# Shorter sine arguments, grouped sines and fewer rotary products in the first stage of a hybrid encoder layer

## The chip, the cores and the metric

The kernel runs on one core of one Trainium2 chip. The core has a matrix engine (PE, with its weight loads, PEld), a vector engine (DVE), a scalar engine that evaluates functions (ACT), a general engine (POOL), and a queue that issues most transfers (SP). Each engine takes its instructions in order. The metric is the device time of one execution in microseconds. Times of single instructions and stages are from one profiled execution; the comparison is between medians of several executions.

## The reference

One encoder layer over 2048 tokens of width 1024. After an RMS norm, one projection gives queries, keys and values of a grouped-query attention with 8 query heads and 2 key heads of 64, and the three streams of a Hyena operator of width 512. Then come the output projection, a residual, an MLP with squared ReLU of width 4096, a residual and a last norm. Two parts matter here. Queries and keys are normalised by head and turned by an axial rotary table:

```
def _rotate(x, cos, sin):
    x1, x2 = jnp.split(x, 2, axis=-1)
    ...
    return jnp.concatenate([x1 * cos - x2 * sin, x2 * cos + x1 * sin], axis=-1)
```

And the long filters of the Hyena operator come from a small network with three sine layers of width 64, evaluated at 2048 positions:

```
    h = jnp.sin(freq * (z @ w1 + b1))
    h = jnp.sin(freq * (h @ w2 + b2))
    h = jnp.sin(freq * (h @ w3 + b3))
    h = h @ w4
```

The frequencies are large enough that the arguments leave the range of one turn, so each has to be brought back to it.

## The kernel before

The kernel is a chain of stages that each free their memory for the next: `qkv_proj` with the filter network beside it; `attention` with the filter's taps and the Hyena projection beside it; the transforms of the filters; two convolutions; the output mix; the MLP. The transforms, the convolutions and the mix run in the order in which they are written (`in_order`). **The first two stages don't:** a builder that models the durations of the instructions gives each engine its order, and an instruction that is ready by the model may be placed ahead of one that stands earlier in the program.

`qkv_proj` goes over 16 token tiles of 128. A tile is loaded and squared for its norm (L204), scaled (L206), turned by eight transposes (L215), split into a high and a low half (`ah` by ACT, L217, `al` by DVE, L218), and multiplied with the split weights: 24 matmuls of 512 columns for the queries, 24 of 256 columns for keys and values (L164 to L166). `taken` copies the result out of the accumulator (L233 to L240), and POOL multiplies it with the gains and with the cosines (L245, L247). `norm_rope` sums the squares by head (L252), takes the reciprocal root (`rstd_steps`, L114 to L121, with a square root on ACT, L116), multiplies the swapped halves with the sines (L259, four products of 160 elements), adds them (L261), scales (L262) and splits (L264 on ACT, L265 on DVE). `finish` turns queries and keys (L279), copies them out on ACT (`qs`, L281) and stores them (L287). The steps of several tiles overlap.

Beside this runs `filter_hidden`, a generator that the loop over tiles pumps once a tile. Its 16 steps each make one argument of 128 partitions by 512 positions: a matmul (L1239), then `sin_argument` on DVE. There the bias is added and the frequency multiplied (L1197), the number of turns is rounded by adding and subtracting a large constant (L1198, L1200), the turns are subtracted in two parts (L1202, twice), and the result is clamped (L1203). `sines` (L1234) runs on ACT over four arguments at a time: four of the first layer, four of the second, twice four of the third. The last layer's results are split into `hc` (L1263 on ACT, L1264 on DVE). Arguments and sines share the six buffers of the tile `sx`.

ACT holds the tables of one set of functions. Where it changes from the square root to the sine or back, the trace has an ACT_TABLE_LOAD.

After the loop, SP issues the loads of the next stage, among them the keys (L422), small vectors of the convolution (L336, L339) and the weights of the Hyena projection (L357). Attention then adds up the weights of each block on POOL (`sum`, L489). Late in that stage, POOL and DVE also fold the taps for the transform (L1398, L1399) as soon as they are loaded back (L1381).

Of the kernel before, what the change touches and what calls it, by code (L numbers as in the profile page):

```python
# [14 lines left out]
AF = mybir.ActivationFunctionType  # L15
ALU = mybir.AluOpType
# [4 lines left out]
P = 128  # L21
# [16 lines left out]
def f32(ap):  # L38
    return ap.bitcast(F32)
# [85 lines left out]
def rstd_from_root(*args):  # L125
    got = []
    pump(rstd_steps(*args, got), 3)
    return got[0]
# [43 lines left out]
def qkv_proj(k, pa, ps, side):  # L172
    nc, a = k.nc, k.a
    x, w_in = a["x"][0], a["w_in"][0]
# [54 lines left out]
    NH = NQ + NKV  # L229
# [20 lines left out]
    def norm_rope(t, y, z, w, cs):  # L250
        ss = pa.tile([P, NH], F32, name="ss")
        nc.vector.tensor_reduce(out=ss[:], in_=z[:], axis=AX.X, op=ALU.add)  # L252
        r = rstd_from_root(k, pa, ss[:], HD, NH, "qr")
        yv = y[:].rearrange("p h (a b e) -> p h a b e", a=2, b=2)
        zv = z[:].rearrange("p h (a b e) -> p h a b e", a=2, b=2)
        sv = cs[:, 1].rearrange("p (a b e) -> p a b e", a=2, b=2)
        for ax in range(2):
            for b in range(2):
                nc.vector.tensor_mul(out=zv[:, :, ax, b], in0=yv[:, :, ax, 1 - b],  # L259
                                     in1=sv[:, ax, b].unsqueeze(1).to_broadcast([P, NH, 16]))  # L260
        nc.vector.tensor_add(out=w[:], in0=w[:], in1=z[:])  # L261
        nc.vector.tensor_mul(out=w[:], in0=w[:], in1=r[:].unsqueeze(2).to_broadcast([P, NH, HD]))  # L262
        hl = pa.tile([P, NH, 2, HD], F32R, name="hl", bufs=FL)
        nc.scalar.copy(out=hl[:, :, 0], in_=w[:])  # L264
        nc.vector.tensor_sub(out=hl[:, :, 1], in0=w[:], in1=f32(hl[:, :, 0]))  # L265
        return hl
# [32 lines left out]
    for i in range(-1 - XL, NT + FL):  # L299
        if i == 13:  # L300
            k.first = load_q(k, 0), {(0, b): load_k(k, k.early, 0, b, 4) for b in range(2)}, load_v(k, k.early, 0)
        if 1 < i + XL + 2 < NT:
            xt[i + XL + 2] = load_x(i + XL + 2)
        e = i - FL
        ending = 0 <= e < NT
        if ending:
            finish(e, *hl[e], 0)
        if 1 < i < NT:
            oq[i] = project(*aT[i], 0, QW)
        if ending:  # L310
            finish(e, *hl[e], 1)
        if 0 <= i + 1 < NT:
            aT[i + 1] = turned(i + 1, xs.pop(i + 1))
        if 0 <= i + XL + 1 < NT:
            xs[i + XL + 1] = normed(i + XL + 1, xt.pop(i + XL + 1))
        if 0 <= i + 1 < 2:
            oq[i + 1] = project(*aT[i + 1], 0, QW)
        pump(side, 1 if i > 0 else 0)
        if ending:
            finish(e, *hl.pop(e), 2)  # L320
        if 0 <= i < NT:
            okv = project(*aT.pop(i), QW, 256)
        if 0 <= i - 1 < NT:
            hl[i - 1] = twice(norm_rope(i - 1, *yz.pop(i - 1)))
        if 0 <= i < NT:
            yz[i] = taken(i, oq.pop(i), okv)
# [859 lines left out]


MAGIC = 1.5 * 2.0 ** 23
TWO_PI = (6.28125, 0.0019353071795864769)
PI_IN = 3.1415925  # L1190


def sin_argument(k, pool, ps, bias, freq):
    nc = k.nc
    x = pool.tile([P, 512], F32, name="sx", bufs=6)
    n = pool.tile([P, 512], F32, name="sn", bufs=2)
    nc.vector.tensor_scalar(out=x[:], in0=ps, scalar1=bias, scalar2=freq, op0=ALU.add, op1=ALU.mult)  # L1197
    nc.vector.tensor_scalar(out=n[:], in0=x[:], scalar1=1.0 / (2.0 * math.pi), scalar2=MAGIC,  # L1198
                            op0=ALU.mult, op1=ALU.add)
    nc.vector.tensor_scalar(out=n[:], in0=n[:], scalar1=MAGIC, scalar2=None, op0=ALU.subtract)  # L1200
    for c in TWO_PI:
        nc.vector.scalar_tensor_tensor(out=x[:], in0=n[:], scalar=-c, in1=x[:], op0=ALU.mult, op1=ALU.add)  # L1202
    nc.vector.tensor_scalar(out=x[:], in0=x[:], scalar1=PI_IN, scalar2=-PI_IN, op0=ALU.min, op1=ALU.max)  # L1203
    return x


# [3 lines left out]
def filter_hidden(k, f1, ps):  # L1210

    nc, a = k.nc, k.a
    H = FH
    w1 = f1.tile([66, P], F32, name="w1")
    w2 = f1.tile([P, P], F32, name="w2")
    w3 = f1.tile([P, 2, P], F32, name="w3")
    fb = f1.tile([P, 3], F32, name="fb")
    fr = f1.tile([P, 1], F32, name="fr")
    for t in (w1, w2, w3):
        nc.gpsimd.memset(t[:], 0.0)  # L1220
    for i in range(2):
        h = slice(i * H, (i + 1) * H)
        nc.sync.dma_start(out=w1[33 * i:33 * (i + 1), h], in_=a["filt_w1"][0])
        nc.sync.dma_start(out=w2[h, h], in_=a["filt_w2"][0])
        for j in range(2):
            nc.sync.dma_start(out=w3[h, i, j * H:(j + 1) * H], in_=a["filt_w3"][0])
        for j, b in enumerate(("filt_b1", "filt_b2", "filt_b3")):
            nc.sync.dma_start(out=fb[h, j:j + 1], in_=a[b][0].unsqueeze(1))
        nc.sync.dma_start(out=fr[h], in_=a["filt_freq"][0].unsqueeze(1))
    yield  # L1230

    def sines(args):
        for x in args:
            nc.scalar.activation(out=x[:], in_=x[:], func=AF.Sin)  # L1234
        return args

    def argument(lhsT, rhs, bias):
        o = ps.get("fl", "fo")
        nc.tensor.matmul(o[:], lhsT, rhs, start=True, stop=True)  # L1239
        return sin_argument(k, f1, o[:], bias, fr[:])  # L1240

    args = []
    for b in range(4):
        z = f1.tile([66, 512], F32, name="z", bufs=2)
        nc.sync.dma_start(out=z[:], in_=a["zT"][:, b * 512:(b + 1) * 512])
        args.append(argument(w1[:], z[:], fb[:, 0:1]))
        yield
    hid = sines(args)
    args = []
    for b in range(4):  # L1250
        args.append(argument(w2[:], hid[b][:], fb[:, 1:2]))
        yield
    hid = sines(args)
    for b0 in range(0, 4, 2):
        args = []
        for b in (b0, b0 + 1):
            for i in range(2):
                args.append(argument(w3[:, i], hid[b][:], fb[:, 2:3]))
                yield
        for n, h3 in enumerate(sines(args)):  # L1260
            b, i = b0 + n // 2, n % 2
            s = slice(b * 512, (b + 1) * 512)
            nc.scalar.copy(out=k.hc[:, i, s], in_=h3[:])  # L1263
            nc.vector.tensor_sub(out=k.hc[H:, i, s], in0=h3[H:], in1=f32(k.hc[H:, i, s]))  # L1264
# [489 lines left out]
def encoder_layer(tc, a):  # L1754
    with ExitStack() as ctx:
        k = setup(tc, ctx, a)
        with sbuf(k, "hid") as hid, sbuf(k, "early") as k.early:
            k.hc = hid.tile([P, 2, SEQ], F32R, name="hc")
            with sbuf(k, "p1", 2) as p1, sbuf(k, "f1") as f1:
                with Banks(k, "ps1", {"tp": 2, "qk": 3, "tq": 2, "fl": 1}) as ps:  # L1760
                    qkv_proj(k, p1, ps, filter_hidden(k, f1, ps))
            with sbuf(k, "at") as at, sbuf(k, "up") as up:
                with Banks(k, "ps2", {"st": 2, "sc": 3, "o": 1, "u": 2}) as ps:
                    taps = taps_ahead(k, ps)
                    attention(k, at, ps, chain(islice(spaced(taps, 1), 16), mixed(taps, MA, u_proj(k, up, ps), MB)))
        with sbuf(k, "wa") as k.wa:
            with Banks(k, "ps3", {"s": 4}, {"x": 2}) as ps:
                with sbuf(k, "hp") as hp:
                    side = att_part(k, hp, ps, list(range(NT)))
                    with sbuf(k, "fd") as fd:  # L1770
                        mix_setup(k, fd)
                        with in_order(tc):
                            filter_dft(k, fd, ps, side)
                    with sbuf(k, "cv") as cv, in_order(tc):
                        conv(k, 0, cv, ps, side)
                        conv(k, 1, cv, ps, side)
                with sbuf(k, "mo") as mo:
                    mlp = mlp_in(k, mo, ps)
                    with sbuf(k, "mx") as mx, in_order(tc):
                        mix(k, mo, mx, ps, k.wo1, mlp)  # L1780
                    with sbuf(k, "mi") as k.mi:
                        pump(mlp)
        with sbuf(k, "out") as out, Banks(k, "ps5", {"y": 8}) as ps:
            mlp_out(k, out, ps)
# [18 lines left out]
```

## Time and profile before

| | |
|---|---|
| time, median of 3 runs (lowest, highest) | 3157.62 us (3154.59, 3162.08) |
| profiled execution, whole | 3165.88 us |
| its span, first to last instruction | 3164.1 us |
| PE, DVE, ACT, POOL busy over the span | 94%, 65%, 45%, 54% |
| mean granted PE clock | 0.975 |
| 16 sines (L1234), first and last start | 59.3 and 228.5 us |
| last store of keys (L287) | 229.6 us |

Shares over the whole span are a mean over stages with different limits. A stage is read from its own windows and from what its engines wait for. In a row of the timeline stand start, duration, engine, line, operation, result and operands, and in brackets the idle time of the engine before it with what ended it. A row of the groups has the count, the busy time in us and the mean in ns.

### The profile page before, as it was taken

How to read it: one execution, taken by the hardware profiler on the slowest of the kernel's cores; microseconds unless marked ns; L12 is line 12 of the kernel's file. 1: busy time of each engine (PE TensorE's matmuls, PEld its weight loads, DVE VectorE, ACT ScalarE, POOL GpSimd, SP SyncE). 2: the span in 40 equal slices, each digit the busy share in tenths (PEclk: the TensorE clock that was granted, in tenths of full speed). 3: DMA queues.
4: the chain of work that ended last, by engine and by line, in shares of the span. 5: the costliest groups of instructions: out<-in, count | busy, mean ns of one | idle time of the engine just before them, and what ended most of it. 6: DMA issues, size and time to landing. Idle time of an engine off the chain costs nothing.

```text
span 3164.1 us, 40514 instructions
## 1 busy us (share of the span) xinstructions
PE 2989.5 (94%) x13400; PEld 2251.3 (71%) x13400; DVE 2048.8 (65%) x3153; ACT 1423.2 (45%) x2626; POOL 1715.1 (54%) x1399
## 2 busy tenths in 40 slices
PE   8978999999998998999999988999999989999998
PEld 6755666666665666676667766888788778888887
DVE  7987777666665554777465567778877535454455
ACT  7866655555553444444444563333433223223333
POOL 3434777778776876244555326777876635250010
PEclk9988999999998999999999998999999999999999
DMA  7758334324334425776656784445644395333454
GB/s 226 221 155 232 115 125 159 110 95 151 125 107 108 140 80 163 263 248 218 186 172 197 253 290 157 156 154 174 204 158 151 121 316 171 133 115 129 146 181 153
DMA packets 482462, 534.45 MB, mean 169 GB/s; under 512 B 49604, under 2 KB 344004, under 8 KB 475212
## 3 DMA queue, kind: packets, MB, share of 16 engines
q1 hardware_dynamic: 464540, 513.16, 50.4%
q0 software_dynamic: 4480, 14.68, 1.3%
q10 hardware_dynamic: 13232, 4.01, 0.6%
q8 instruction: 107, 1.75, 0.2%
q14 instruction: 103, 0.84, 0.1%
HBM read 326.22 MB, written 198.19 MB: 166 GB/s over the span
## 4 chain that ended last, share of the span: by engine, by line
PE 75%; DVE 5%; DMA 5%; issue 3%; POOL 3%; ACT 2%; SPq 1%; ACTq 0%; POOLq 0%; DVEq 0%
PE o L502 7%; PE y L164 6%; PE y L165 6%; PE y L166 6%; PE g L166 5%; PE g L165 5%; PE g L164 5%; PE st L481 4%; PE X L1435 4%; PE st L482 3%; PE sc L461 3%; PE uo L164 3%; PE uo L165 2%; PE uo L166 2%; PE b L1565 2%
## 5 line engine op out<-in xcount | busy, mean ns | idle before, releaser
L489 POOL TENSOR_TENSOR sum<-sum,p 128x512 f32<-128x512 f32 x416 | 552.9, 1329 | 125.3 <-ACT p L484 98.9
L464 DVE TENSOR_REDUCE top<-sc 128x1 f32<-128x512 f32 x512 | 347.4, 687 | 255.4 <-PE sc L461 252.3
L484 ACT ACTIVATE p<-st 128x512 f32<-128x512 f32 x512 | 303.2, 597 | 317.6 <-PE st L482 299.9
L164 PE MATMUL g<-mh,wop 128*128 128x512 f32 x896 | 350.5, 391 | 17.9 <-ACT wop L914 17.6
L165 PE MATMUL g<-ml,wop 128*128 128x512 f32 x896 | 350.6, 391 | 2.8 <-DVE ml L925 2.8
L166 PE MATMUL g<-mh,wop 128*128 128x512 f32 x896 | 350.4, 391 | 2.4 <-DVE wop L915 2.4
L164 PE MATMUL y<-bh,ah 128*128 128x512 f32 x768 | 299.8, 391 | 15.5 <-ACT bh L1082 15.5
L1091 DVE TENSOR_TENSOR ah<-ar,ah 128x1024 fp32r<-128x1024 f32 x111 | 148.9, 1342 | 235.2 <-ACT ah L1090 232.9
L165 PE MATMUL y<-bh,ah 128*128 128x512 f32 x768 | 299.7, 390 | 0.0
L166 PE MATMUL y<-bh,ah 128*128 128x512 f32 x768 | 299.7, 390 | 0.0
L1090 ACT CAST ah<-ar 128x1024 fp32r<-128x1024 f32 x111 | 117.0, 1054 | 347.8 <-PE y L166 343.0
L502 PE MATMUL o<-p,vt 128*64 128x512 f32 x1024 | 234.9, 598 | 0.0
L461 PE MATMUL sc<-kt,q 128*128 128x512 f32 x512 | 208.0, 410 | 15.0 <-DVE top L464 11.9
L481 PE MATMUL st<-q,kt 128*128 128x512 f32 x512 | 215.0, 420 | 1.6 <-ACT p L484 1.4
L164 PEld LDWEIGHTS g<-mh,wop 128*128 128x128 f32 x896 | 169.2, 189 | 54.2 <-ACT wop L914 18.0
L482 PE MATMUL st<-q,kt 128*128 128x512 f32 x512 | 203.8, 398 | 0.0
L165 PEld LDWEIGHTS g<-ml,wop 128*128 128x128 f32 x896 | 169.0, 189 | 38.9 <-DVE ml L925 3.9
L166 PEld LDWEIGHTS g<-mh,wop 128*128 128x128 f32 x896 | 169.1, 189 | 38.4 <-DVE wop L915 3.5
L914 ACT CAST wop<-ws 128x512 fp32r<-128x512 f32 x128 | 79.1, 621 | 223.5 <-PE g L166 192.1
L164 PEld LDWEIGHTS y<-bh,ah 128*128 128x128 f32 x768 | 144.7, 189 | 46.2 <-ACT bh L1082 15.9
L166 PEld LDWEIGHTS y<-bh,ah 128*128 128x128 f32 x768 | 144.7, 188 | 30.3
L165 PEld LDWEIGHTS y<-bh,ah 128*128 128x128 f32 x768 | 144.7, 188 | 30.2 <-DVE bh L1083 0.2
(306 smaller groups left out, 7054.6 us busy)
## 6 DMA issues: line engine op xcount, KB each, us to landing
ar<-H_d SPq DMA_DIRECT2D x111, 512.0 KB, 3.8
uw<-uw_d SPq DMA_DIRECT2D x36, 1024.0 KB, 5.0
w1raw<-in_w_mlp_in SPq DMA_DIRECT2D x64, 512.0 KB, 4.2
H_d<-r SPq DMA_DIRECT2D x96, 256.0 KB, 2.2
H_d<-s SPq DMA_DIRECT2D x96, 256.0 KB, 2.0
F_d<-F SPq DMA_DIRECT2D x34, 512.0 KB, 3.2
F<-F_d SPq DMA_DIRECT2D x34, 512.0 KB, 4.6
aT<-aT_d SPq DMA_DIRECT2D x32, 512.0 KB, 6.6
```

The lines of the kernel that those rows point to most:

```text
L164: mm(out, l_hi, r_hi, start=start, stop=False)
L165: mm(out, l_hi, r_lo, start=False, stop=False)
L166: mm(out, l_lo, r_hi, start=False, stop=stop)
L461: nc.tensor.matmul(s[:], u.q[:, h], kt[u.kv, b][0][:], start=True, stop=True)
L464: nc.vector.tensor_reduce(out=u.top[:, h, b:b + 1], in_=s[:], axis=AX.X, op=ALU.max, negate=True)
L481: nc.tensor.matmul(s[:], lo[:, c], u.q2[:].rearrange("p h t -> p (h t)"), start=True, stop=False)
L482: nc.tensor.matmul(s[:], hi[:, c], u.q[:].rearrange("p h t -> p (h t)"), start=False, stop=True)
L484: nc.scalar.activation(out=p[:], in_=s[:], func=AF.Exp)
L489: nc.gpsimd.tensor_add(out=u.sum[:], in0=u.p0[:] if j == 1 else u.sum[:], in1=p[:])
L502: nc.tensor.matmul(u.o[cols], vt[j // 8][:, j % 8, u.kv], p[:], start=j < 2, stop=j > 13)
L1091: nc.vector.tensor_sub(out=h[:, 1], in0=raw[:], in1=f32(h[:, 0]))
L1435: k.nc.tensor.matmul(d[:, ri], t[:, m], Af[:, 2 * j + at], start=True, stop=True)
```

## The change

There are three edits. `fr`, the frequency, is divided by two pi once, so that the argument comes out in turns; it is rounded by one operation with two constants, the rounded turns are subtracted, and the sine gets the factor of two pi as its scale; the clamp goes. The four sines of a group become one section that the builder can't break up. And in `norm_rope` one product with the halves read in reverse takes the place of two.

```
         for ax in range(2):
-            for b in range(2):
-                nc.vector.tensor_mul(out=zv[:, :, ax, b], in0=yv[:, :, ax, 1 - b],
-                                     in1=sv[:, ax, b].unsqueeze(1).to_broadcast([P, NH, 16]))
+            nc.vector.tensor_mul(out=zv[:, :, ax], in0=yv[:, :, ax, ::-1],
+                                 in1=sv[:, ax].unsqueeze(1).to_broadcast([P, NH, 2, 16]))
...
-TWO_PI = (6.28125, 0.0019353071795864769)
-PI_IN = 3.1415925
+TURN = 6.283185
...
     nc.vector.tensor_scalar(out=x[:], in0=ps, scalar1=bias, scalar2=freq, op0=ALU.add, op1=ALU.mult)
-    nc.vector.tensor_scalar(out=n[:], in0=x[:], scalar1=1.0 / (2.0 * math.pi), scalar2=MAGIC,
-                            op0=ALU.mult, op1=ALU.add)
-    nc.vector.tensor_scalar(out=n[:], in0=n[:], scalar1=MAGIC, scalar2=None, op0=ALU.subtract)
-    for c in TWO_PI:
-        nc.vector.scalar_tensor_tensor(out=x[:], in0=n[:], scalar=-c, in1=x[:], op0=ALU.mult, op1=ALU.add)
-    nc.vector.tensor_scalar(out=x[:], in0=x[:], scalar1=PI_IN, scalar2=-PI_IN, op0=ALU.min, op1=ALU.max)
+    nc.vector.tensor_scalar(out=n[:], in0=x[:], scalar1=MAGIC, scalar2=MAGIC, op0=ALU.add, op1=ALU.subtract)
+    nc.vector.tensor_sub(out=x[:], in0=x[:], in1=n[:])
     return x
...
+    nc.vector.tensor_scalar_mul(out=fr[:], in0=fr[:], scalar1=1.0 / (2.0 * math.pi))
     yield

     def sines(args):
-        for x in args:
-            nc.scalar.activation(out=x[:], in_=x[:], func=AF.Sin)
+        with k.tc.tile_critical():
+            for x in args:
+                nc.scalar.activation(out=x[:], in_=x[:], func=AF.Sin, scale=TURN)
         return args
```

## The prediction

> **What bounds the kernel now.** The page of the profile shows that the change touches only the first stage: the lines of `sin_argument`, `sines` and `norm_rope` all run before 231 us of the 3164.1. So I read that stage alone, first as busy time by windows. The columns are the window, then busy us and count of PE, PEld (weight loads), DVE, ACT and POOL, then the granted PE clock and DMA.
>
> ```profile
> core 0: us, PE busy (x) PEld busy (x) DVE busy (x) ACT busy (x) POOL busy (x), PEclk, DMA share, GB/s
> ...
> 110.00:130.00 20.00, 20.00 (x113) 16.30 (x113) 18.52 (x45) 16.44 (x32) 10.02 (x10) 0.94 0.81 251
> 130.00:150.00 20.00, 17.87 (x110) 14.78 (x109) 17.70 (x40) 15.33 (x30) 7.10 (x10) 1.00 0.63 188
> ...
> 170.00:190.00 20.00, 17.73 (x90) 14.03 (x89) 17.36 (x34) 16.93 (x33) 8.46 (x12) 0.85 0.57 167
> 190.00:209.00 19.00, 19.00 (x118) 16.14 (x117) 18.46 (x38) 11.54 (x21) 8.16 (x9) 0.98 0.45 133
> 209.00:230.00 21.00, 9.36 (x45) 5.46 (x43) 19.07 (x36) 14.14 (x26) 5.79 (x8) 0.72 0.42 127
> ```
>
> There are two parts. Up to 209 us PE and DVE are both near full. From 209 to 230 us only DVE is: PE has no projection left and the stage drains. The busy share does not say which of PE and DVE binds before 209, so I took the period of a token tile next, from ACT's timeline: one squaring L204 starts each tile.
>
> ```profile
> 63.12 1.28 ACT L116 ACT_TABLE_LOAD   x1
> 64.42 0.20 ACT L116 ACTIVATE rstde<-rstdy 128x1 f32<-128x1 f32 x1
> 64.64 1.28 ACT L1234 ACT_TABLE_LOAD   x1
> 66.66 0.63 ACT L1234 ACTIVATE sx<-sx 128x512 f32<-128x512 f32 x1 [0.74 <-DVE sx L1203]
> ...
> 85.25 1.12 ACT L204 ACTIVATE xs<-xt 128x1024 f32<-128x1024 f32 x1
> ...
> 148.34 1.11 ACT L204 ACTIVATE xs<-xt 128x1024 f32<-128x1024 f32 x1
> ```
>
> Five tiles lie between the last two rows: (148.34 - 85.25) / 5 = 12.6 us each. What PE needs for a tile is read from start to start in its timeline, as its durations overlap.
>
> ```profile
> 125.06 0.39 PE L164 MATMUL qkv<-wh,ah 128*128 128x512 f32 x1
> ...
> 126.88 0.39 PE L166 MATMUL qkv<-wh,al 128*128 128x512 f32 x1
> 127.11 0.45 PE L279 MATMUL tq<-identr,hl 128*128 128x128 f32 x4
> ...
> 132.38 0.46 PE L279 MATMUL tq<-identr,hl 128*128 128x128 f32 x4
> 132.69 0.50 PE L164 MATMUL qkv<-wh,ah 128*128 128x512 f32 x1
> ...
> 134.59 0.50 PE L166 MATMUL qkv<-wh,al 128*128 128x512 f32 x1 [1.17 <-DVE al L218]
> ...
> 146.11 0.54 PE L279 MATMUL tq<-identr,hl 128*128 128x128 f32 x4 [0.96 <-ACT qs L281]
> ```
>
> Eight steps from 125.06 to 126.88 give 0.228 us per 512-column matmul, so 24 of them 5.5. Transposes, the filter's matmul and the 24 narrow ones take 132.38 - 127.11 = 5.3, the last transposes 0.3. Together 11.1 us. So PE waits about 1.5 us of each 12.6 us tile, on DVE (`al`) and on ACT (`qs`), and **that is all the change can take off a tile**. Between the first sine at 59 us and the last projection at 209 us lie 150 / 12.6 = 12 tiles: a ceiling of 18 us there.
>
> **The change, part by part.** DVE's work first, grouped by line and form from 50 to 230 us (busy us, mean ns of one, then idle time before).
>
> ```profile
> L1202 DVE SCALAR_TENSOR_TENSOR sx<-sn,sx 128x512 f32<-128x512 f32 x32 | 28.1, 878 | 0.3
> L259 DVE TENSOR_TENSOR z<-y,cs 128x160 f32<-128x160 f32 x56 | 17.4, 333 | 0.0
> ...
> L1197 DVE TENSOR_SCALAR sx<-fo,fb,fr 128x512 f32<-128x512 f32 x16 | 12.9, 804 | 0.0
> ...
> L261 DVE TENSOR_TENSOR w<-w,z 128x640 f32<-128x640 f32 x14 | 11.5, 825 | 1.2
> ...
> L1200 DVE TENSOR_SCALAR sn<-sn 128x512 f32<-128x512 f32 x16 | 9.8, 611 | 0.3
> L1198 DVE TENSOR_SCALAR sn<-sx 128x512 f32<-128x512 f32 x16 | 9.5, 593 | 0.1
> L1203 DVE TENSOR_SCALAR sx<-sx 128x512 f32<-128x512 f32 x16 | 6.7, 418 | 0.1
> ```
>
> *Arguments.* L1197 stays, and the rounding in one operation has the form of L1198. The sine's added scale is a constant; I give L1234 its 0.63 us as before. L1200, L1203 and one of two L1202 go; the subtraction in place of the other L1202 has its shape and its two inputs, so I give it the same 878 ns. That is 611 + 418 + 878 = 1907 ns per argument, 30.5 us over 16. Part of these means is time lost to other work; undisturbed rows of the tail give the lower end:
>
> ```profile
> 224.69 0.43 DVE L1200 TENSOR_SCALAR sn<-sn 128x512 f32<-128x512 f32 x1
> ...
> 227.29 0.69 DVE L1202 SCALAR_TENSOR_TENSOR sx<-sn,sx 128x512 f32<-128x512 f32 x1
> 228.01 0.43 DVE L1203 TENSOR_SCALAR sx<-sx 128x512 f32<-128x512 f32 x1
> ```
>
> That is 1.55 us, 25 us over 16. About one argument falls to a tile: 1.9 us, at least 1.5.
>
> *Rotary products.* Four of 333 ns become two of 320 elements. No row has that form; between 333 ns at 160 and 825 ns at 640 elements lies 497 ns, so 1.33 us becomes 0.99: 0.3 us a tile. If reading the halves in reverse made each as dear as the 640-element form, it would be 1.65, a loss of 0.3; that is the other end.
>
> *Scaling of `fr`.* One 128x1 operation, once, below any row above. L1197 reads `fr` anyway, so it waits for the same loads.
>
> DVE, busy 17.7 of 20 us or 11.2 of a tile, falls to 9.0, clearly under PE's 11.1. PE then binds.
>
> *Sines.* ACT's groups in the first 420 us, and its longest wait of that kind:
>
> ```profile
> L1234 ACT ACT_TABLE_LOAD x14 | 18.0, 1283 | 0.2
> ...
> L116 ACT ACT_TABLE_LOAD x13 | 16.7, 1283 | 0.2
> ```
>
> ```profile
> ACT qre L116 <- DVE qry L114: 16.7, 6, 4.6
> ```
>
> Sine and square root take turns on ACT, each with a load (63.12 to 66.66 above). Four unbreakable sections need four sine loads and about four back: 27 - 8 = 19 fewer, 19 x 1.283 = 24.4 us, 2 us of ACT's 9.7 in a tile (15.33 of 20 us, times 12.6). ACT is not the bound, so this pays only as a shorter wait for `qs`, `ah` and the root; if PE's and DVE's cover were gone it would be worth 2 us a tile. The Trainium skill, "ScalarE: Activation LUTs", What ACT_TABLE_LOAD costs, puts a switch at 1283 ns plus about 1380 ns of draining; by it 19 switches would be 50.5 us. The trace agrees with the load but not with the drain: the next activation starts 1.30 us after the load does.
>
> Against this stands a new wait: the section starts when its fourth argument is ready. Behind it in ACT's order stand `ah` and `qs` copies, for which PE waits. I take 1 us a section, as the row 66.66 shows 0.74 for a sine that waited for its one argument, and leave it inside the half that the sum below gives away; its ends are nothing and the 4.6 us of the row above. A second wait goes with it: `sx` has six buffers, and the four of arguments 9 to 12 now come free only after their section, so argument 13 waits for all four sines and casts, about 4 x 2 x 0.63 = 5 us. A tile of 12.6 us separates one argument from the next, which hides it; without that cover it would cost the 5 us once.
>
> **Sum.** To 209 us I take half of the 18, about 8.5: DVE at 9.0 of 11.1 us still makes PE wait at times, since queues are in order. Ends: 0 and 18. In the drain three arguments lie on DVE: 3 x 1.55 + 0.4 (rope of the last tile) = 5.0 off, and this is on the path:
>
> ```profile
> 228.01 0.44 DVE sx L1203
> ...
> 229.01 0.58 ACT qs L281
> ...
> 229.60 4.05 DMA k_d<-qs
> ...
> 241.74 6.65 SPq L339
> ```
>
> The last key store waits for a copy that stands behind the last sine on ACT. With the last section ahead of it there are four sines of 0.63 us (row 66.66) in place of one: 1.9 back at worst. I take 4; the ends are 5, if nothing comes back, and -1.9, if the drain is not DVE's after all. Attention's loads are issued by SP in order after that store, so what is late next is the same chain, earlier by the whole. Together 12.5 us. The profiled run took 3165.88 us around its span of 3164.1; less 12.5 that is 3153.4. The median, 8.3 lower, becomes **3157.6 - 12.5 = 3145.1 us**.
>
> **The rivals.**
>
> *Only the drain gains.* PE's 1.5 us come from order, not from DVE's load, and stay. For it: PE is at 20.00 of 20 in one window. Against: the waits are named, on DVE and ACT. 3157.6 - 4 = 3153.6. It stands here too if the section breaks up and the loads stay.
>
> *PE is not the bound.* Then a tile shortens by all of DVE's 2.2 us: 12 x 2.2 + 5 = 31, so 3126. Against: matmuls without a gap at 0.228 us. The Trainium skill, "Perfetto Trace Analysis", Identifying the Most-Contended Engine, says busy matmul time is a poor measure of headroom and weight-load time a better one; with PEld at 14.78 of 20 us that rule leaves a quarter of PE free.
>
> *Attention is reordered.* The stage after is ordered by the builder too, and its order is redrawn. One load stops it now:
>
> ```profile
> 975.53 13.80 DMA x<-taps_d
> ```
>
> POOL's fold waits there for the taps, and the sums of attention behind it. That wait may go or come twice: 3145 -+ 14, so 3131 or 3159.
>
> *The sections block ACT: slower.* Each holds ACT for 4.6 us of waiting plus 1.28 of load, and PE with it: 4 x 5.9 = 23.5, so 3168.6. It turns the result at about 3 us a section. For it: arguments are stretched in ways the builder can't foresee (878 against 690 ns for L1202). Against: ACT is idle a quarter of the time.
>
> **How the numbers follow.** Forecast 0.50; drain only 0.18; PE not the bound 0.07; wait gone 0.06, wait twice 0.07; sections block 0.12. A measurement can tell about 0.2%, 6.3 us: below 3151.3 is faster, above 3163.9 slower. Faster: 0.48 of the forecast, 0.07 and 0.06 = 0.61. Same: 0.02 + 0.18 + 0.07 = 0.27. Slower: 0.12. The range from 3131 to 3160 leaves out the blocked sections and the unbound PE, 0.19.
>
> **What would show it.** Right: eight or so table loads before 230 us instead of 27; DVE near 80% of a tile; a tile period of 11.7 to 12.0; the last key store near 217. Wrong: PE's waits for `al` and `qs` as long as now; ACT idle before L1234's successor by 3 us or more; a longer stop than 14 us at the fold; a store at 217 but the end unmoved.

## The result, and the profile after

| | before | after |
|---|---|---|
| time, median (lowest, highest) of 9 runs each | 3159.16 us (3154.59, 3164.59) | 3168.56 us (3165.4, 3175.81) |
| ratio after / before, 95% interval | | 1.003 (1.0018 to 1.0042) |
| profiled execution, its span | 3165.88, 3164.1 us | 3165.4, 3163.6 us |
| start of the last projection matmul (L166) | 208.92 us | 222.42 us |
| last store of keys | 229.6 us | 241.0 us |

The change made the kernel **slower by 9.4 us, or 0.3%**; 3145.1 had been predicted. The two spans are nearly equal because before was profiled in a run 6.7 us above its median and after in one 3.2 below its own. So the stage is compared, not the span: its last key store lies 241.0 - 229.6 = 11.4 us later, about what the medians differ by. One execution each of two kernels below, of 5010.54 and 8782.27 us, ran in a slower state of the chip and is left out of its median.

The windows of after, with the columns as in the prediction:

```profile
core 0: us, PE busy (x) PEld busy (x) DVE busy (x) ACT busy (x) POOL busy (x), PEclk, DMA share, GB/s
110.00:130.00 20.00, 20.00 (x126) 17.32 (x125) 14.88 (x34) 14.03 (x31) 7.23 (x12) 1.00 0.84 251
130.00:150.00 20.00, 16.60 (x93) 12.56 (x92) 10.21 (x23) 11.71 (x23) 5.40 (x7) 0.92 0.48 140
...
209.00:230.00 21.00, 15.72 (x95) 11.96 (x94) 19.88 (x40) 10.31 (x25) 9.86 (x13) 1.00 0.58 173
```

The first row is the one that was promised: DVE 14.88 of 20 us where it was 18.52, PE without a gap. In the second row every engine is less busy than before, PE 16.60 instead of 17.87, DVE 10.21 instead of 17.70, ACT 11.71 instead of 15.33, and DMA moves 140 GB/s instead of 188. No engine is full there. In the last row PE is still at 15.72; in before the projections were over by then.

What they wait for stands in ACT's groups up to 420 us (count, busy us, mean ns, then the idle time before):

```profile
L1231 ACT ACT_TABLE_LOAD x4 | 5.1, 1283 | 15.3 <-DMA k_d<-qs 8.0 <-PE tp L215 5.8 <-DVE hl L264 1.5
L116 ACT ACT_TABLE_LOAD x3 | 3.8, 1283 | 0.1
```

The loads fell from 27 to 7. But ahead of the four loads that open the four sections ACT was idle for **15.3 us**; before the change it was 0.2 us ahead of fourteen. None of the three names is an argument of a sine: a store of keys, a transpose of PE (L215) and a split of DVE (L264), of which no sine reads anything. An entry waits for many semaphores at once, and the view names the one that moved last; which of them held it is read further down.

The timeline around the first section:

```profile
81.97 0.74 SPq L220 DMA_DIRECT2D aT_d<-al  x1
...
82.50 0.61 ACT L280 CAST qs<-tq 128x512 fp32r<-128x512 f32 x1
...
83.14 1.45 SPq L286 DMA_DIRECT2D k_d<-qs  x1
...
83.33 0.67 DVE L1198 TENSOR_TENSOR sx<-sx,sn 128x512 f32<-128x512 f32 x1
...
87.37 1.28 ACT L1231 ACT_TABLE_LOAD   x1 [4.15 <-DMA k_d<-qs]
...
88.67 2.19 ACT L1231 ACTIVATE sx<-sx 128x512 f32<-128x512 f32 x4
...
92.47 0.29 ACT L240 ACTIVATE z<-qkv 128x128 f32<-128x128 f32 x1
92.49 0.46 POOL L245 TENSOR_TENSOR y<-y,qkg 128x128 f32<-128x128 f32 x1 [10.51 <-ACT y L234]
...
92.79 0.82 DVE L252 TENSOR_REDUCE ss<-z 128x10 f32<-128x640 f32 x1 [8.33 <-ACT z L240]
```

The fourth argument is ready at 83.33 + 0.67 = 84.00. ACT starts the section only at 87.37. Behind the section in ACT's order stand the copies of a finished projection (L234, L240), and DVE and POOL have nothing else left: they stand still for 8.33 and 10.51 us.

The compiled order of ACT's instructions in after says why. L1796 is no line of the computation; it is the branch into another block of instructions.

```
L116 ACTIVATE rstde<-rstdy 128x1 [waits DVE_49]
L1229 NO_OP [waits DVE_49]
L1796 UNCONDITIONAL_BRANCH [waits DMAHW2_49,DMAHW1_49,DMAHW3_49,DMAHW0_49,DMAHW4_49,Activation_sequencer_49,DMAHW5_49,DVE_49,DMAHW6_49,PE_49,DMAHW7_49,Activation_49,Pool_49]
L1231 ACT_TABLE_LOAD
L1231 ACTIVATE sx<-sx 128x512 x4
L1229 UNCONDITIONAL_BRANCH
L1229 NO_OP [waits Activation_49,Activation_sequencer_49]
L206 ACTIVATE xs<-xt,rstd 128x1024 [waits DVE_49,Activation_49]
```

The section is a block of its own. Its entry waits for eight semaphores of transfers and for those of PE, DVE, POOL and ACT, and the trace has these waits one after another ahead of each of the four loads. The trace's records of these semaphores say what held ACT. In the first entry the two waits that take longest end at 85.44 and 87.04, when the two stores of the split norm (`aT_d`, L220) land that SP issued at 81.26 and 81.97. In the second and third entry the store of the low half, issued at 137.90 and 193.42, lands at 142.46 and 198.76, just ahead of the loads at 143.01 and 199.31. The key stores that SP issued next, at 83.14, 139.07 and 193.87, land at 87.84, 143.17 and 199.49, when the loads have already started. In the fourth entry, the shortest, no landing ends the wait. So the entry waited for transfers that no sine reads, though not for every transfer in flight.

Part of the 15.3 us is the wait for the fourth argument itself. The four were ready at 84.00, 139.93, 195.30 and 232.46, in all 3.6 us after ACT had gone idle. The other 11.7 us passed with the argument ready.

The section's exit waits for ACT's own work: the exit's drain lasts 2.1 us in the trace, until the four sines are through.

```profile
L1229 ACTq DRAIN  x4: 2117/2117/2132, 88.8 to 235.0; - x4
```

DVE's waits between 50 and 231 us add up what this does to its neighbours (us in total, times, longest), in after:

```profile
DVE ss L252 <- ACT z L240: 23.5, 6, 8.3
```

### The profile page after: what moved, and what is told of

The parts are those of the page before. It is cut to its first block, busy times and chain, and to the rows that moved or that the text cites. A ratio compares the mean times of both kernels' runs of the same rounds, so it can differ in the third digit from the quotient of the medians.

```text
span 3163.6 us, 40476 instructions
## 1 busy us (share of the span) xinstructions
PE 2989.2 (94%) x13400; PEld 2253.5 (71%) x13400; DVE 2013.9 (64%) x3074; ACT 1397.8 (44%) x2606; POOL 1702.3 (54%) x1399
## 4 chain that ended last, share of the span: by engine, by line
PE 41%; DMA 3%; issue 2%; POOL 2%; DVE 1%; ACT 1%; SPq 0%; ACTq 0%; POOLq 0%; DVEq 0%
PE y L164 6%; PE y L166 6%; PE y L165 6%; PE g L166 6%; PE g L165 6%; PE g L164 6%; PE X L1432 1%; PE b L1562 1%; DMA ml<-sb 1%; PE yo L1627 1%; PE cs L1529 1%; ACT sb L789 0%; DVE sb L801 0%; DMA mo_d<-sb 0%; PE bt L1586 0%
## 5 line engine op out<-in xcount | busy, mean ns | idle before, releaser
L166 PE MATMUL g<-mh,wop 128*128 128x512 f32 x896 | 350.6, 391 | 2.4 <-DVE wop L914 2.4
L166 PE MATMUL y<-bh,ah 128*128 128x512 f32 x768 | 299.9, 391 | 0.0
L166 PEld LDWEIGHTS g<-mh,wop 128*128 128x128 f32 x896 | 169.2, 189 | 38.3 <-DVE wop L914 3.5
L166 PEld LDWEIGHTS y<-bh,ah 128*128 128x128 f32 x768 | 144.9, 189 | 30.0
```

The lines of the kernel that those rows point to most:

```text
L166: mm(out, l_lo, r_hi, start=False, stop=stop)
```

## The experiments

The theory after the first look: the section's boundary costs the time, and the shorter arguments and products gain what they were to gain. The rivals: the cost is the four sines in a row or their order (the body of the section), the shorter operations gain nothing, or a reordered attention takes it back. All ratios are to before, on the same chip. Where two kernels come from different chips, their ratios are subtracted and multiplied by 3160 us; such a difference is uncertain by about 5 us (half-widths of 0.0012 twice, root of the squares 0.0017). Line numbers of a kernel shift by a few from one to the next.

**The change without the section.**

```
-        with k.tc.tile_critical():
-            for x in args:
-                nc.scalar.activation(out=x[:], in_=x[:], func=AF.Sin, scale=TURN)
+        for x in args:
+            nc.scalar.activation(out=x[:], in_=x[:], func=AF.Sin, scale=TURN)
```

> The changed kernel with the four sines as single instructions again; its DVE edits stay. Theory A (the section holds ACT until all transfers and engines behind it have reported, and drains it: about 8 us each): the last key store moves from 241.0 to about 219 us, some 27 table loads come back, and the time is 3148 to 3152 against 3159 of before. Theory B (the shorter arguments gain nothing, since PE binds): last key store near 229, time 3157 to 3161. Theory C (the loss is in a redrawn attention, not in the sections): the stage ends as in the changed kernel and the time stays near 3168.

3144.69 us, ratio 0.9943 (0.9931 to 0.9955): one line taken away turns 0.3% slower into 0.6% faster. Last key store at 219.5, not 241.0. The table loads are back, and ACT no longer waits ahead of them:

```profile
L1230 ACT ACT_TABLE_LOAD x15 | 19.2, 1283 | 0.3
...
L116 ACT ACT_TABLE_LOAD x14 | 18.0, 1283 | 0.2
```

DVE's wait for `z` is 3.4 us, not 23.5, in the same view:

```profile
DVE ss L252 <- ACT z L240: 3.4, 2, 1.7
```

**The section alone**, on before's sines.

```
-        for x in args:
-            nc.scalar.activation(out=x[:], in_=x[:], func=AF.Sin)
+        with k.tc.tile_critical():
+            for x in args:
+                nc.scalar.activation(out=x[:], in_=x[:], func=AF.Sin)
```

> The kernel before with nothing but the section around the four sines; arguments and rotary products as before. Theory A: the sections cost about 20 us and nothing gives any of it back, so the last key store comes after 241 us, at about 248, and the time is about 3177. Theory B (sections cost all the 9 us, DVE edits gain nothing): 3168. Theory C: within 0.2% of 3159.

3173.71 us, 1.0036 (1.0023 to 1.0048); last key store at 240.4, 10.8 later than before's 229.6 and short of the 248 that theory A gave. So the section costs time without the other edits too. Its entries waited 9.8 us, of which 3.7 passed before an argument was ready (the twelfth, at 197.86, with ACT idle from 194.19):

```profile
L1235 ACT ACT_TABLE_LOAD x4 | 5.1, 1283 | 9.8 <-DMA q_d<-qs 8.9 <-DVE qr L118 0.5 <-DMA q<-q_d 0.3
```

**The rotary products alone**, on before.

```
-            for b in range(2):
-                nc.vector.tensor_mul(out=zv[:, :, ax, b], in0=yv[:, :, ax, 1 - b],
-                                     in1=sv[:, ax, b].unsqueeze(1).to_broadcast([P, NH, 16]))
+            nc.vector.tensor_mul(out=zv[:, :, ax], in0=yv[:, :, ax, ::-1],
+                                 in1=sv[:, ax].unsqueeze(1).to_broadcast([P, NH, 2, 16]))
```

> The kernel before with the two reversed products in place of four, nothing else. By the prediction's term 0.3 us of DVE a tile: between 0 and 4 us faster, last key store between 225 and 230 us. If reversed halves were slow: up to 4 us slower.

3157.51 us, 0.9979 (0.9969 to 0.9989), about 6.6 us where 0 to 4 were expected. The stage shows little of it: the last projection starts at 206.58, against 208.92 and 208.25 in two profiles of before, and the last key store at 229.1 against 229.6. Where the rest comes from is not settled.

**The arguments alone**, with the division of `fr` and the sine's scale, neither section nor rotary edit.

```
-    nc.vector.tensor_scalar(out=n[:], in0=x[:], scalar1=1.0 / (2.0 * math.pi), scalar2=MAGIC,
-                            op0=ALU.mult, op1=ALU.add)
...
-    nc.vector.tensor_scalar(out=x[:], in0=x[:], scalar1=PI_IN, scalar2=-PI_IN, op0=ALU.min, op1=ALU.max)
+    nc.vector.tensor_scalar(out=n[:], in0=x[:], scalar1=MAGIC, scalar2=MAGIC, op0=ALU.add, op1=ALU.subtract)
+    nc.vector.tensor_sub(out=x[:], in0=x[:], in1=n[:])
...
-            nc.scalar.activation(out=x[:], in_=x[:], func=AF.Sin)
+            nc.scalar.activation(out=x[:], in_=x[:], func=AF.Sin, scale=TURN)
```

> The kernel before with the short arguments and the scaled sine alone: no section, four rotary products as before. If the arguments carry the gain as the sum of the prediction had it (1.9 of 2.2 us a tile): 3146 to 3150 beside 3159 of before. If the rotary products carried as much as their own run showed: 3151 to 3154.

3146.62 us, 0.9955 (0.9943 to 0.9966); last key store at 221.6. That is 8.0 of the 10.1 us by which the stage is shorter with both edits and no section, so most of the gain is this edit's.

**Four sines in one instruction.** The four arguments of a group are written into one tile, and one activation takes them all: one load for four sines, with no section. The rest is the change's.

```
+    def group():
+        return f1.tile([P, 4, 512], F32, name="sx", bufs=2)
+
+    def sines(g):
+        nc.scalar.activation(out=g[:], in_=g[:], func=AF.Sin, scale=TURN)
+        return [g[:, j] for j in range(4)]
```

> The changed kernel without the section; the four arguments of a group lie in one tile of 128x2048 and one activation takes all four, so the loads stay at four for sines and four back, with no boundary. Theory A: the grouping itself gains, so at least as fast as the kernel with single sines: 3143 to 3149, last key store 213 to 219, ACT waits for the fourth argument by under 2 us a group. Rival: waiting for the fourth argument is what costs, not the boundary: 3160 or more, with ACT idle by 4 us or more before each wide sine.

3144.78 us, 0.9945 (0.9931 to 0.9958), last key store at 218.0. ACT's groups:

```profile
L1230 ACT ACTIVATE sx<-sx 128x2048 f32<-128x2048 f32 x4 | 7.7, 1916 | 0.5 <-DVE sx L1197 0.5
...
L1230 ACT ACT_TABLE_LOAD x4 | 5.1, 1283 | 0.1
...
L116 ACT ACT_TABLE_LOAD x3 | 3.8, 1283 | 0.1
```

Here stand the loads that the section was to bring, 7 and not 29, and with a wait of 0.6 us. The time is that of the kernel with 29 loads, and the stage ends 1.5 us earlier. So 22 loads, 28 us of ACT, and the wait for the fourth argument that came in their place weigh next to nothing together. DVE waits here too for the copies behind a sine, in the same view as above:

```profile
DVE ss L252 <- ACT z L240: 14.8, 7, 2.7
```

The total is nearer to the 23.5 us of after than to the 3.4 us of single sines, yet the kernel is as fast as the latter. The longest wait, 2.7 us against 8.3, tells the kernels apart; the total does not.

**The same on before**, with its old arguments: one wide sine in place of four, no section.

```
-        for x in args:
-            nc.scalar.activation(out=x[:], in_=x[:], func=AF.Sin)
-        return args
+        nc.scalar.activation(out=g[:], in_=g[:], func=AF.Sin)
+        return [g[:, j] for j in range(4)]
```

> The kernel before with the four arguments of a group in one tile and one activation for all four, arguments and rotary products as before. Nineteen table loads fewer on ACT, 24 us of it. If ACT is off the path: within 0.2% of before, 3153 to 3165. If the loads sat in the path through the reciprocal root and the copies: 3145 to 3152.

3157.67 us, 0.9986 (0.9976 to 0.9996): 20 loads fewer than before and at most a few us gained, while the stage ended later (last key store at 233.1). The wait for the fourth argument costs nothing large either.

**The wide sine inside a section.** Now the body is a single instruction, which needs no section.

```
     def sines(g):
-        nc.scalar.activation(out=g[:], in_=g[:], func=AF.Sin, scale=TURN)
+        with k.tc.tile_critical():
+            nc.scalar.activation(out=g[:], in_=g[:], func=AF.Sin, scale=TURN)
```

> The kernel with one wide activation a group, and that activation inside the section. What stands in the section is one instruction of 1.92 us instead of four of 2.19, and without the section this kernel takes 3144.8. If the boundary's wait is the cost, the time returns to that of the changed kernel: 3162 to 3172, with ACT idle for 2 to 6 us before each load. If four sines in one piece were the cost: 3144 to 3149.

3169.64 us, 1.0026 (1.0016 to 1.0035): 26 us slower than the same kernel without it (0.0081 of 3160 by the ratios), last key store 240.4 against 218.0. What the engine waited for ahead of L1231, from the view of that line (us, times):

```profile
  PE tp L215: 6.1, 1
  DMA k_d<-qs: 3.9, 1
  DMA aT_d<-al: 3.7, 1
  DVE hl L264: 1.5, 1
```

Here the view of the first entry names the store `aT_d<-al`. The body is the same as in the kernel without the section, and in ACT's timeline the copies of the projection stand behind the sine in both. The source differs by the section alone. The builder's order changes a little with it: the scaling L206 follows the first sine's copies without the section (87.02) and precedes them with it (90.83). This is the run that shows most directly that the section costs the time, and not the sines in one piece.

**Only the first group in a section.**

```
-    def sines(args):
-        with k.tc.tile_critical():
+    def sines(args, whole=False):
+        with ExitStack() as c:
+            if whole:
+                c.enter_context(k.tc.tile_critical())
...
-    hid = sines(args)
+    hid = sines(args, True)
```

> The changed kernel with the section around the first group of four sines only; the other twelve are single. Four sections cost 3168.6 - 3144.7 = 23.9 us, so by theory A (a price for each entry) one costs about 6: 3149 to 3153, and the last key store stands near 225 us. Rival (the first section starts a new order in which the later ones cost nothing, or only the last one, in the drain, costs): 3160 or more, or under 3147.

3151.91 us, 0.997 (0.9958 to 0.9982): 8.5 us above the kernel without a section (0.9970 - 0.9943 of 3160), last key store at 225.2, which is 5.7 later. One section out of four takes about a quarter to a third.

**Almost empty sections**: single sines as without a section, and then a section that holds only the copy of one column of the last sine into a tile that nobody reads.

```
+        for x in args:
+            nc.scalar.activation(out=x[:], in_=x[:], func=AF.Sin, scale=TURN)
         with k.tc.tile_critical():
-            for x in args:
-                nc.scalar.activation(out=x[:], in_=x[:], func=AF.Sin, scale=TURN)
+            nc.scalar.copy(out=cr[:], in_=args[3][:, 0:1])
```

> The changed kernel with the sixteen sines single, and after each group of four a section that holds nothing but a copy of one column of the last sine (its result is not used). Theory A (the boundary costs, not what stands in it): as slow as the changed kernel or slower, 3165 to 3173, with ACT idle by some 4 us before each copy. Rival (what costs is that four sines and a load in one piece keep ACT from its copies): within 3 us of the kernel without sections, 3144 to 3148.

3148.9 us, 0.9958 (0.9946 to 0.9971): only 4.7 us above no section by the ratios, inside the uncertainty, and 2.2 us in the stage. **A price per section, the same wherever it stands, fell with this run.** The rival's number is nearly met, but four sines in one piece cost nothing without a section (3144.78 above), so the rival alone does not hold either. What ACT waited for ahead of the four copies:

```profile
  DMA cs<-in_rope: 2.0, 1
  DVE w L261: 1.9, 1
  DVE qr L121: 1.5, 1
  POOL kk L270: 0.6, 1
```

6.0 us in all, and the drain on leaving is 0.12 us, with one short copy to wait for. The names are again those of the semaphore that moved last.

**The same section ahead of the sines**, copying a column of the fourth argument.

```
         with k.tc.tile_critical():
-            for x in args:
-                nc.scalar.activation(out=x[:], in_=x[:], func=AF.Sin, scale=TURN)
+            nc.scalar.copy(out=cr[:], in_=args[3][:, 0:1])
+        for x in args:
+            nc.scalar.activation(out=x[:], in_=x[:], func=AF.Sin, scale=TURN)
```

> As with the empty sections, but each stands ahead of its group's sines and copies a column of the fourth argument, so it is entered when the section of the changed kernel is: as soon as the fourth argument is there. The sines are single. If the price of a boundary is what is in flight where it stands: waits of 3 to 6 us before the copies and 3156 to 3168, unlike the 3148.9 of the sections behind the sines. If an almost empty section is cheap wherever it stands: 3146 to 3151.

3153.17 us, 0.9975 (0.9964 to 0.9987), between the two expectations; last key store at 227.2. Its waits:

```profile
  DVE w L260: 4.9, 1
  DVE z L258: 2.9, 1
  DVE qr L118: 0.8, 1
  DVE w L261: 0.4, 1
```

9.0 us. In the third entry (4.9 us) the argument was ready 1.1 us after ACT had gone idle, and then three stores, of which the copy reads nothing, landed at 190.01, 190.75 and 190.95. In the first (2.9 us) nothing that the trace names ends the longest step, so what held it stays open. Put together, against the kernel with the same operations and no section:

| sections | entry waits, us | of it with the argument ready | last key store, later by | time, by the ratios |
|---|---|---|---|---|
| four, almost empty, behind the sines | 6.0 | 6.0 | 2.2 | +4.7 |
| one, with four sines | 4.2 | 3.5 | 5.7 | +8.5 |
| four, almost empty, ahead of the sines | 9.0 | 7.9 | 7.7 | +10 |
| four with four sines, old arguments | 9.8 | 6.1 | 10.8 | +11 |
| four with a wide sine | 15.2 | 11.6 | 22.4 | +26 |
| four with four sines (the change) | 15.3 | 11.7 | 21.5 | +27 |

In the four kernels whose sections hold the sines, a us of wait with the argument ready goes with 1.6 to 1.9 us of stage (5.7 / 3.5 to 22.4 / 11.6). Where a section holds next to nothing it is 2.2 / 6.0 = 0.4 and 7.7 / 7.9 = 1.0. So the price is not the entry's wait alone: a section that holds the load and the sines as well is dearer. Why is not shown. A likely reason is that the load, the sines and the exit keep ACT's copies from DVE and POOL after these have run dry in the wait.

**Before again**, unchanged, for a second profile.

> The kernel before once more, for a second profile. From its last key store to its last store of attention it took 991.8 us in the first profile, the nine others took 985 to 994. If that was the run and not the order of the instructions: about 986 here, and the stage itself ends within 2 us of 229.6. If before's order of attention is the slower one: again 990 to 994.

3158.49 us, 0.9995 (0.9984 to 1.0007). The last key store is at 229.6 in both profiles, so the stage repeats well; the last store of attention's result is at 1217.4 where the first profile has 1221.4. Attention's 991.8 us in the first profile of before (from 229.6 to 1221.4) are 987.8 in the second and 1228.9 - 241.0 = 987.9 in after. It was not reordered in a way that costs or gains. Of the others, the wide sine on before took 1215.4 - 233.1 = 982.3, below the 985 that the expectation names as their lowest.

## Why the prediction was wrong

**The step that failed is "the section starts when its fourth argument is ready".** The term "I take 1 us a section" rests on it and prices the wait for that argument alone. That much was about right: 3.6 us over the four, 0.9 a section. What the sum put at nothing is the wait for everything else that the entry asks for, transfers of other tiles above all: 11.7 us over the four, with the argument ready. Together it was 15.3 / 4 = 3.8 us a section, above the point of "about 3 us a section" from which the section was said to turn the result. The row 66.66 was the wrong neighbour, because it showed a sine that waits for one argument; before has no row of an entry into a block. The upper end, 4.6 us, held for the mean and for three of the four waits, which were 4.15, 3.87, 5.77 and 1.51. The rival "the sections block ACT" gave 3168.6 and the median came to 3168.56, at a chance of 0.12. Its direction is right, but that it met the number is luck: it took 4 x 5.9 us of waiting and loading as so much time lost, while 15.3 us of waiting and 5.1 of loading went with a stage that ends 21.5 us later than without the section.

Against the prediction's list, "ACT idle before L1234's successor by 3 us or more" came true, as did the eight or so loads; the store "near 217" did not.

The other steps, read in the kernels without a section:

*Up to the last projection* 8.5 us were predicted, half of the ceiling. Measured: 208.92 - 202.14 = 6.8 with single sines (6.1 against the second profile of before), 208.92 - 200.37 = 8.6 with the wide one (7.9). The size is right. The wait that was named gave part of it: PE's waits for `al` and `qs`, from 50 us to the last projection, were 8.5 us before (9.6 in its second profile), 5.3 with single sines and 5.1 with the wide one. The tile period came out at 11.9 us with the wide sine, (165.77 - 70.70) / 8 by ACT's squarings, inside the 11.7 to 12.0 named:

```profile
70.70 1.11 ACT L204 ACTIVATE xs<-xt 128x1024 f32<-128x1024 f32 x1
...
165.77 1.09 ACT L204 ACTIVATE xs<-xt 128x1024 f32<-128x1024 f32 x1
```

With single sines the squarings are still 12.4 us apart, so the gain does not show in them there. In after the same view has this:

```profile
81.46 1.09 ACT L204 ACTIVATE xs<-xt 128x1024 f32<-128x1024 f32 x1
...
100.66 1.09 ACT L204 ACTIVATE xs<-xt 128x1024 f32<-128x1024 f32 x1
...
137.39 1.09 ACT L204 ACTIVATE xs<-xt 128x1024 f32<-128x1024 f32 x1
...
156.69 1.11 ACT L204 ACTIVATE xs<-xt 128x1024 f32<-128x1024 f32 x1
```

19.2 and 19.3 us for the tiles into which the first two sections fall, where the wide sine has 13.3 and 12.3.

*The drain*: 4 predicted. From the last projection to the last key store before took 229.6 - 208.92 = 20.7 us, the kernel without sections 219.5 - 202.14 = 17.4: 3.3. The size is right.

*Durations.* DVE's groups from 50 to 230 us, without the section:

```profile
L258 DVE TENSOR_TENSOR z<-y,cs 128x320 f32<-128x320 f32 x28 | 12.7, 488 | 0.0
...
L1198 DVE TENSOR_TENSOR sx<-sx,sn 128x512 f32<-128x512 f32 x16 | 11.7, 732 | 0.2
...
L1197 DVE TENSOR_SCALAR sn<-sx 128x512 f32<-128x512 f32 x16 | 8.8, 551 | 0.0
```

The product that lies between two known widths took 488 ns where 497 was estimated, so reading the halves in reverse cost nothing that shows beside the estimate. The subtraction took 732 ns, not 878: the edit is a little better than costed.

*Loads off the path*: right. The load itself is 1283 ns everywhere, and with 22 fewer the time is the same (3144.69 and 3144.78 us).

*The wait for a free `sx` buffer* in argument 13: no row of after shows DVE waiting for it.

*The other rivals.* "Only the drain gains" fell: the last projection starts 6.8 us earlier without the section. "PE is not the bound" fell: DVE was relieved by what was costed, and the stage became 10 to 12 us shorter, not 31. "Attention is reordered" fell, by the three lengths of attention above.

*The sum.* 12.5 us were forecast for a change whose sections cost next to nothing. That kernel exists here, the one with the wide sine. Its stage ends 229.6 - 218.0 = 11.6 earlier, and its ratio 0.9945 is 17 us. The few us beyond the stage stay open. Between key store and the end of the span lie 3142.6 - 218.0 = 2924.6 us there, 2923.4 in the change without a section, 2927.4 and 2934.5 in two profiles of before, and 2922.6 in after. A single profile of each can't tell such a difference from the scatter of a kernel's own runs, and no run here was made for it.

The fastest versions are the change without the section (3144.69) and with one wide sine for four (3144.78). They can't be told apart, and both beat before and after; the first is the smaller edit.

## What to carry to other kernels

A section that the scheduler can't break up is not a hint on order but a block with a barrier at its entry: ask what other engines and transfers still have to finish where it stands, and not only when its own operands are ready. Where instructions are to stay together, one instruction over a wider tile does it without a boundary. And when three edits come as one change, time them apart: one line here hid a gain of 0.6% behind a loss of 0.9%.

## What the runs showed of the hardware and the builder

The entry of a section waited for the landing of stores that its body has nothing to do with (`aT_d`, issued at 81.97 and landed at 87.04, with the load at 87.37 and the argument ready at 84.00). The exit drained ACT for 2.1 us after four sines and 0.12 us after a copy of one column. A wide sine of 2048 columns took 1916 ns, against 4 x 632 = 2528 ns for four single ones of 512 in the kernel without a section; inside a section, back to back, four took 2.19 us. And with 22 table loads of 1283 ns fewer, 28 us of an engine's time, the time was the same in the two fastest kernels.

A profile that puts a wait for several semaphores down to one of them can name the wrong one: the view named the key store issued at 83.14, which landed at 87.84, after the wait had ended.
